# Local attention over windows of 64: q and k loaded as float32 by SyncE, transposed as float32 and cast when PSUM is emptied; 256 rows per transfer; manual program order

## The chip, the cores and the metric

One NeuronCore of a Trainium2 chip. The metric is device time in microseconds (us), the median of several executions; lower is better. One core runs alone. (Mean granted TensorE clock: the share of the full clock that the profile shows as granted.) The kernel before takes 966.62 us (966.24 to 967.0).

## The reference

```python
B, S, D, W = 4, 4096, 1536, 64            # q, k, v: float32, (B, S, D)
q_w, k_w, v_w = (x.reshape(B, S // W, W, D) for x in (q, k, v))
logits = einsum('bnwd,bnud->bnwu', q_w, k_w) * D ** -0.5
attn = softmax(logits)                    # over the last axis
out = einsum('bnwu,bnud->bnwd', attn, v_w).reshape(B, S, D)   # float32
```

The 16,384 rows are 128 blocks of 128 rows (two windows each). Whatever a kernel does, it must read 301.99 MB of q, k and v from HBM, the memory outside the core, and write 100.66 MB: 402.65 MB in all, 3.146 MB per block. SBUF and PSUM, below, are the core's own memories; in both kernels TensorE's results go to PSUM and are copied from there ("evicted") to SBUF.

## The kernel before

The parts that the change and the argument touch (pool lines shortened, cuts at "..."):

```python
inp = tile_pool(name="inp", bufs=3); outp = tile_pool(name="outp", bufs=6)
tp_ps = tile_pool(name="tp_ps", bufs=2, space=PSUM)
# lt_ps bufs=2, o_ps bufs=3, s_ps bufs=1

def load(blk):                       # 128 rows; float32 in HBM, float16 in SBUF: the transfer casts
    ...
    nc.gpsimd.dma_start(out=q16, in_=qb[blk].rearrange("p (c e) -> p c e", e=128))
    nc.gpsimd.dma_start(out=k16, in_=kb[blk].rearrange("p (c e) -> p c e", e=128))
    nc.gpsimd.dma_start(out=v16, in_=vb[blk])
    return q16, k16, v16
...
for blk in range(NBLK):
    ... load(blk) ...
    if len(pending_store) > 2:
        bs, ts = pending_store.pop(0)
        nc.gpsimd.dma_start(out=ob[bs], in_=ts)
    for g in range(3):               # 24 transposes: d onto the partitions
        tp = tp_ps.tile([128, 8, 128], FP16, tag="tp", name="tp")
        for i in range(8):
            ...
            nc.tensor.transpose(tp[:, i, :], src, ident)
        if g != 1:
            nc.vector.tensor_copy(out=xt[:, g * 8 : g * 8 + 8, :], in_=tp)
        else:
            nc.scalar.copy(out=xt[:, g * 8 : g * 8 + 8, :], in_=tp)
    # ... 12 score matmuls, exp on the two 64x64 diagonal tiles, row sums, reciprocal
    for j in range(D // 512):        # values, two 64-row matmuls side by side, then scaled into out_sb
        ...
```

All loads and stores (but the last three stores) go through one queue, GpSimd's. A scheduler orders the instructions.

The softmax here doesn't subtract the row's maximum and nothing guards it: scores larger than these inputs give would overflow.

Of the kernel before, what the change touches and what calls it, by code (L numbers as in the profile page):

```python
# [1 line left out]

# [4 lines left out]

FP16 = mybir.dt.float16
FP32 = mybir.dt.float32  # L10


@with_exitstack
def kernel(
    ctx: ExitStack,
    tc: tile.TileContext,
    q: bass.AP,
    k: bass.AP,
    v: bass.AP,
    out: bass.AP,  # L20
):
    nc = tc.nc

    B, S, D, W = q.shape[0], q.shape[1], q.shape[2], 64
    P = 128
    DC = D // 128
    NBLK = (B * S) // P
    scale = float(D) ** -0.5
    NPRE = 2

    qb = q.rearrange("b (n p) d -> (b n) p d", p=P)
    kb = k.rearrange("b (n p) d -> (b n) p d", p=P)
    vb = v.rearrange("b (n p) d -> (b n) p d", p=P)
    ob = out.rearrange("b (n p) d -> (b n) p d", p=P)

    consts = ctx.enter_context(tc.tile_pool(name="consts", bufs=1))
    inp = ctx.enter_context(tc.tile_pool(name="inp", bufs=3))
    xtp = ctx.enter_context(tc.tile_pool(name="xtp", bufs=2))
    etp = ctx.enter_context(tc.tile_pool(name="etp", bufs=2))
    outp = ctx.enter_context(tc.tile_pool(name="outp", bufs=6))  # L40
    rsp = ctx.enter_context(tc.tile_pool(name="rsp", bufs=2))

    tp_ps = ctx.enter_context(tc.tile_pool(name="tp_ps", bufs=2, space=bass.MemoryType.PSUM))
    lt_ps = ctx.enter_context(tc.tile_pool(name="lt_ps", bufs=2, space=bass.MemoryType.PSUM))
    o_ps = ctx.enter_context(tc.tile_pool(name="o_ps", bufs=3, space=bass.MemoryType.PSUM))
    s_ps = ctx.enter_context(tc.tile_pool(name="s_ps", bufs=1, space=bass.MemoryType.PSUM))

    exp_f = mybir.ActivationFunctionType.Exp
    copy_f = mybir.ActivationFunctionType.Copy

    def load(blk):
        q16 = inp.tile([128, DC, 128], FP16, tag="q16", name="q16")
        k16 = inp.tile([128, DC, 128], FP16, tag="k16", name="k16")
        v16 = inp.tile([128, D], FP16, tag="v16", name="v16")
        nc.gpsimd.dma_start(out=q16, in_=qb[blk].rearrange("p (c e) -> p c e", e=128))  # L55
        nc.gpsimd.dma_start(out=k16, in_=kb[blk].rearrange("p (c e) -> p c e", e=128))  # L56
        nc.gpsimd.dma_start(out=v16, in_=vb[blk])  # L57
        return q16, k16, v16

    pre = [load(blk) for blk in range(NPRE)]  # L60
    pending_store = []

    ident = consts.tile([128, 128], FP16, name="ident")
    ones = consts.tile([128, 8], FP16, name="ones")
    zeros = consts.tile([128, 1], FP32, name="zeros")
    nc.vector.memset(ident, 0.0)
    nc.vector.memset(ones, 1.0)
    nc.vector.memset(zeros, 0.0)
    nc.gpsimd.affine_select(
        out=ident,  # L70
        in_=ident,
        compare_op=mybir.AluOpType.not_equal,
        fill=1.0,
        base=0,
        pattern=[[-1, 128]],
        channel_multiplier=1,
    )

    for blk in range(NBLK):
        if blk < NPRE:  # L80
            q16, k16, v16 = pre[blk]
        else:
            q16, k16, v16 = load(blk)
        if len(pending_store) > 2:
            bs, ts = pending_store.pop(0)
            nc.gpsimd.dma_start(out=ob[bs], in_=ts)  # L86

        xt = xtp.tile([128, 2 * DC, 128], FP16, tag="xt", name="xt")
        for g in range(3):
            tp = tp_ps.tile([128, 8, 128], FP16, tag="tp", name="tp")  # L90
            for i in range(8):
                j = g * 8 + i
                c = j // 2
                src = q16[:, c, :] if (j % 2 == 0) else k16[:, c, :]
                nc.tensor.transpose(tp[:, i, :], src, ident)  # L95
            if g != 1:
                nc.vector.tensor_copy(out=xt[:, g * 8 : g * 8 + 8, :], in_=tp)  # L97
            else:
                nc.scalar.copy(out=xt[:, g * 8 : g * 8 + 8, :], in_=tp)  # L99

        lt = lt_ps.tile([128, 512], FP32, tag="lt", name="lt")
        for c in range(DC):
            nc.tensor.matmul(  # L103
                lt[:, 0:128],
                lhsT=xt[:, 2 * c + 1, :],
                rhs=xt[:, 2 * c, :],
                start=(c == 0),
                stop=(c == DC - 1),
            )

        et = etp.tile([128, 128], FP16, tag="et", name="et")
        nc.scalar.activation(  # L112
            et[0:64, 0:64], lt[0:64, 0:64], exp_f, bias=zeros[0:64], scale=scale
        )
        nc.scalar.activation(
            et[64:128, 64:128], lt[64:128, 64:128], exp_f, bias=zeros[64:128], scale=scale
        )

        sp = s_ps.tile([128, 8], FP32, tag="sp", name="sp")
        nc.tensor.matmul(  # L120
            sp[0:64, 0:1], lhsT=et[0:64, 0:64], rhs=ones[0:64, 0:1],
            tile_position=(0, 0), start=True, stop=True,
        )
        nc.tensor.matmul(  # L124
            sp[64:128, 0:1], lhsT=et[64:128, 64:128], rhs=ones[64:128, 0:1],
            tile_position=(64, 64), start=True, stop=True,
        )
        rs = rsp.tile([128, 1], FP32, tag="rs", name="rs")
        nc.vector.reciprocal(out=rs, in_=sp[:, 0:1])  # L129

        out_sb = outp.tile([128, D], FP32, tag="out_sb", name="out_sb")
        for j in range(D // 512):
            o = o_ps.tile([128, 512], FP32, tag="o", name="o")
            sl = slice(512 * j, 512 * (j + 1))
            nc.tensor.matmul(  # L135
                o[0:64, :], lhsT=et[0:64, 0:64], rhs=v16[0:64, sl],
                tile_position=(0, 0), start=True, stop=True,
            )
            nc.tensor.matmul(  # L139
                o[64:128, :], lhsT=et[64:128, 64:128], rhs=v16[64:128, sl],  # L140
                tile_position=(64, 64), start=True, stop=True,
            )
            if j % 2 == 0:
                nc.scalar.activation(out_sb[:, sl], o, copy_f, bias=0.0, scale=rs)  # L144
            else:
                nc.vector.tensor_scalar_mul(out_sb[:, sl], o, scalar1=rs)  # L146

        pending_store.append((blk, out_sb))

    for bs, ts in pending_store:  # L150
        nc.sync.dma_start(out=ob[bs], in_=ts)


# [1 line left out]
_INS = ['q', 'k', 'v']  # L155
_OUTS = [((4, 4096, 1536), 'float32')]


# [23 lines left out]
```

## Time and profile before

| | before |
|---|---|
| time, median | 966.62 us |
| profiled span, mean granted TensorE clock | 964.4 us, 0.632 |
| HBM bytes | 402.65 MB, 417 GB/s over the span |
| HBM bytes in the steady part, 100 to 900 us | 423.6 GB/s |
| last load landed | 955.8 us |

The steady rate is worked out from the trace's records of DMA packets: those that ended between 100 and 900 us, each counted at the size that it has in HBM. A packet is here one row of 1,536 values, moved by one of the 16 DMA engines. A packet of a casting load appears in the records with its float16 size, 3,072 bytes, and is counted as the 6,144 bytes that it reads. The table of stretches agrees: 265 GB/s at the SBUF side, and of the program's bytes 402.65 MB cross HBM for 251.66 MB at that side, so 265 x 1.6 = 424.

The page of the kernel before, its span, two rows of slices (each digit is a fortieth of the span; PEclk is the granted TensorE clock in tenths, DMA the busy share of the 16 DMA engines), the HBM line and the chain of waits:

```profile
span 964.4 us, 14246 instructions
...
PEclk9776575756756666566575755766656556565655
DMA  9999999999999999999999999999999999999997
...
HBM read 301.99 MB, written 100.66 MB: 417 GB/s over the span
...
DMA 94%; issue 4%; PE 1%; POOL 0%; DVE 0%; ACT 0%; POOLq 0%; ACTq 0%; DVEq 0%
DMA k<-in_k_dram 92%; DMA q<-in_q_dram 1%; PE tp L95 1%; DVE xt L97 0%; POOL q L55 0%; PE o L135 0%; PE lt L103 0%; PE o L139 0%; POOLq L56 0%; POOL v L57 0%; DVE out_sb L146 0%; ACT out_sb L144 0%; ACT et L112 0%; ACTq L177 0%; PE sp L120 0%
```

The digits of 9 say that the DMA engines are busy throughout, and the chain, followed back from the last instruction, goes from one k load to the next: the kernel waits for its data and for hardly anything else.

Three groups of instructions of the same page (count, then busy us and mean ns, then idle time of the engine just before and what ended it):

```profile
L95 PE MATMUL tp<-ident,q 128*128 128x128 f16 x1536 | 341.1, 296 | 28.8 <-DMA q<-in_q_dram 12.1
...
L97 DVE COPY xt<-tp 128x1024 f16<-128x1024 f16 x256 | 177.0, 691 | 392.4 <-PE tp L95 392.2
...
L99 ACT COPY xt<-tp 128x1024 f16<-128x1024 f16 x128 | 129.5, 1012 | 287.2 <-PE tp L95 287.2
```

And the DMA issues of that page (count, KB each, median us from issue to landing). The sizes of loads are those at the SBUF side, float16:

```profile
out_dram<-out_sb POOLq DMA_DIRECT2D x125, 768.0 KB, 14.2
q<-in_q_dram POOLq DMA_DIRECT2D x128, 384.0 KB, 14.3
k<-in_k_dram POOLq DMA_DIRECT2D x128, 384.0 KB, 14.3
v<-in_v_dram POOLq DMA_DIRECT2D x128, 384.0 KB, 14.3
```

Every kind of transfer takes the same 14.2 to 14.3 us; all stand in one queue in program order.

The timeline of the kernel before at 13.4 us, with the TensorE clock at full speed (start in us, then duration):

```profile
13.36 0.22 PE L95 MATMUL tp<-ident,q 128*128 128x128 f16 x1
...
13.42 0.22 PE L95 MATMUL tp<-ident,k 128*128 128x128 f16 x1
...
13.48 0.22 PE L95 MATMUL tp<-ident,q 128*128 128x128 f16 x1
```

Start to start, float16 transposes are 0.053 to 0.06 us apart. At the low clock (0.5 of the full one in the records, and granted for 74% of the span) the same timeline shows 0.107.

### The profile page before, as it was taken

To read this page: it belongs to the slowest core of one execution; us is meant where nothing else is said; L and a number is where in the kernel's file an instruction comes from. 1 tells how busy PE (TensorE), PEld (TensorE's weight loads), DVE (VectorE), ACT (ScalarE), POOL (GpSimd) and SP (SyncE) were. 2 spreads that over 40 slices of the span, in tenths; PEclk is the share of its full clock that TensorE was granted. 3 is DMA by queue.
4 is the path that set the end of the run, shared out by engine and by line. 5 is a ranking of instruction groups with operands and counts; after the bars stand their busy time and mean duration, and the time that the engine had idled before them with its cause. 6 is when DMAs were issued, how large, how long until landed. Compare 5 with 4: busy or idle time off the path is not lost.

```text
span 964.4 us, 14246 instructions
## 1 busy us (share of the span) xinstructions
PE 731.4 (76%) x5632; PEld 510.0 (53%) x5632; DVE 294.6 (31%) x515; ACT 378.1 (39%) x641; POOL 271.1 (28%) x514
## 2 busy tenths in 40 slices
PE   5667778787687877877878777777787777878775
PEld 3445555555455555555555555544555555555553
DVE  2323332333333333323233333323332323323332
ACT  3434343433333443434343433344343333344333
POOL 4222222222222222222222322322222222222220
PEclk9776575756756666566575755766656556565655
DMA  9999999999999999999999999999999999999997
GB/s 182 253 270 269 261 261 268 270 262 261 266 270 264 261 266 268 266 262 265 266 267 262 266 264 267 264 266 264 265 267 266 264 264 267 266 264 263 267 268 224
DMA packets 73795, 252.60 MB, mean 262 GB/s; under 512 B 8192, under 2 KB 8192, under 8 KB 73728
## 3 DMA queue, kind: packets, MB, share of 16 engines
q0 software_dynamic: 73296, 249.33, 104.6%
q1 hardware_dynamic: 432, 2.36, 0.6%
q8 instruction: 44, 0.72, 0.3%
q14 instruction: 23, 0.19, 0.0%
HBM read 301.99 MB, written 100.66 MB: 417 GB/s over the span
## 4 chain that ended last, share of the span: by engine, by line
DMA 94%; issue 4%; PE 1%; POOL 0%; DVE 0%; ACT 0%; POOLq 0%; ACTq 0%; DVEq 0%
DMA k<-in_k_dram 92%; DMA q<-in_q_dram 1%; PE tp L95 1%; DVE xt L97 0%; POOL q L55 0%; PE o L135 0%; PE lt L103 0%; PE o L139 0%; POOLq L56 0%; POOL v L57 0%; DVE out_sb L146 0%; ACT out_sb L144 0%; ACT et L112 0%; ACTq L177 0%; PE sp L120 0%
## 5 line engine op out<-in xcount | busy, mean ns | idle before, releaser
L95 PE MATMUL tp<-ident,k 128*128 128x128 f16 x1536 | 327.7, 305 | 139.6 <-DMA k<-in_k_dram 139.6
L95 PE MATMUL tp<-ident,q 128*128 128x128 f16 x1536 | 341.1, 296 | 28.8 <-DMA q<-in_q_dram 12.1
L95 PEld LDWEIGHTS <-k 128*128 128x128 f16 x1536 | 205.9, 139 | 205.3 <-DMA k<-in_k_dram 167.9
L97 DVE COPY xt<-tp 128x1024 f16<-128x1024 f16 x256 | 177.0, 691 | 392.4 <-PE tp L95 392.2
L95 PEld LDWEIGHTS <-q 128*128 128x128 f16 x1536 | 199.8, 137 | 89.8 <-DMA q<-in_q_dram 50.9
L99 ACT COPY xt<-tp 128x1024 f16<-128x1024 f16 x128 | 129.5, 1012 | 287.2 <-PE tp L95 287.2
L144 ACT ACTIVATE out_sb<-o,rs 128x512 f32<-128x512 f32 x256 | 168.6, 685 | 98.7 <-PE o L139 95.1
L103 PE MATMUL lt<-xt 128*128 128x128 f16 x1536 | 192.9, 295 | 3.0 <-DVE xt L97 1.8
L103 PEld LDWEIGHTS <-xt 128*128 128x128 f16 x1536 | 150.6, 136 | 27.4 <-DVE xt L97 26.5
L135 PE MATMUL o<-v,et 64*64 64x512 f16 x384 | 150.6, 502 | 0.0
L139 PE MATMUL o<-v,et 64*64 64x512 f16 x384 | 144.6, 498 | 0.0
L57 POOL DMA_DIRECT2D v<-in_v_dram x128 | 67.9, 530 | 178.1 <-DMA v<-in_v_dram 135.0
L86 POOL DMA_DIRECT2D out_dram<-out_sb x125 | 67.2, 537 | 173.5 <-DMA out_dram<-out_sb 134.0
L112 ACT ACTIVATE et<-lt,zeros 64x64 f16<-64x64 f32 x128 | 39.6, 309 | 192.4 <-PE lt L103 192.4
L56 POOL DMA_DIRECT2D k<-in_k_dram x128 | 67.9, 530 | 162.6 <-DMA k<-in_k_dram 162.6
L55 POOL DMA_DIRECT2D q<-in_q_dram x128 | 68.0, 531 | 156.2 <-PE o L139 124.0
L146 DVE TENSOR_SCALAR out_sb<-o,rs 128x512 f32<-128x512 f32 x128 | 96.0, 750 | 46.6 <-PE o L139 45.1
L129 DVE RECIPROCAL rs<-sp 128x1 f32<-128x1 f32 x128 | 21.5, 168 | 225.5 <-PE sp L124 221.0
L120 PE MATMUL sp<-ones,et 64*64 64x1 f16 x128 | 25.3, 198 | 56.5 <-ACT et L112 56.5
L120 PEld LDWEIGHTS <-et 64*64 64x64 f16 x128 | 14.4, 113 | 86.7 <-ACT et L112 86.2
L139 PEld LDWEIGHTS <-et 64*64 64x64 f16 x384 | 39.4, 132 | 16.8 <-issue 9.8
L135 PEld LDWEIGHTS <-et 64*64 64x64 f16 x384 | 43.5, 126 | 0.4
(12 smaller groups left out, 81.5 us busy)
## 6 DMA issues: line engine op xcount, KB each, us to landing
out_dram<-out_sb POOLq DMA_DIRECT2D x125, 768.0 KB, 14.2
q<-in_q_dram POOLq DMA_DIRECT2D x128, 384.0 KB, 14.3
k<-in_k_dram POOLq DMA_DIRECT2D x128, 384.0 KB, 14.3
v<-in_v_dram POOLq DMA_DIRECT2D x128, 384.0 KB, 14.3
out_dram<-out_sb SPq DMA_DIRECT2D x3, 768.0 KB, 7.8
```

The source lines that it names most:

```text
L55: nc.gpsimd.dma_start(out=q16, in_=qb[blk].rearrange("p (c e) -> p c e", e=128))
L56: nc.gpsimd.dma_start(out=k16, in_=kb[blk].rearrange("p (c e) -> p c e", e=128))
L57: nc.gpsimd.dma_start(out=v16, in_=vb[blk])
L86: nc.gpsimd.dma_start(out=ob[bs], in_=ts)
L95: nc.tensor.transpose(tp[:, i, :], src, ident)
L97: nc.vector.tensor_copy(out=xt[:, g * 8 : g * 8 + 8, :], in_=tp)
L99: nc.scalar.copy(out=xt[:, g * 8 : g * 8 + 8, :], in_=tp)
L103: nc.tensor.matmul(lt[:, 0:128], lhsT=xt[:, 2 * c + 1, :], rhs=xt[:, 2 * c, :], start=(c == 0), stop=(c == DC - 1),)
L135: nc.tensor.matmul(o[0:64, :], lhsT=et[0:64, 0:64], rhs=v16[0:64, sl], tile_position=(0, 0), start=True, stop=True,)
L139: nc.tensor.matmul(o[64:128, :], lhsT=et[64:128, 64:128], rhs=v16[64:128, sl], tile_position=(64, 64), start=True, stop=True,)
L144: nc.scalar.activation(out_sb[:, sl], o, copy_f, bias=0.0, scale=rs)
L146: nc.vector.tensor_scalar_mul(out_sb[:, sl], o, scalar1=rs)
```

## The change

The intent: take the cast out of DMA and q and k off GpSimd's software queue, make transfers twice as large, and lay down the order by hand, with the values of one block after the scores of the next. Its core (cut at "..."):

```diff
+BODY_G, BODY_R = 2, 1        # groups of 128 rows per transfer, rows per partition
+PREFETCH = 3
-    inp = ctx.enter_context(tc.tile_pool(name="inp", bufs=3))
-    outp = ctx.enter_context(tc.tile_pool(name="outp", bufs=6))
+    inp = ctx.enter_context(tc.tile_pool(name="inp", bufs=PREFETCH + 1))
+    outp = ctx.enter_context(tc.tile_pool(name="outp", bufs=3))
...
-        nc.gpsimd.dma_start(out=q16, in_=qb[blk].rearrange("p (c e) -> p c e", e=128))
-        nc.gpsimd.dma_start(out=k16, in_=kb[blk].rearrange("p (c e) -> p c e", e=128))
-        nc.gpsimd.dma_start(out=v16, in_=vb[blk])
+    ctx.enter_context(tc.manual_schedule())
+    def load(u):
+        for name, src in (("q", qf), ("k", kf), ("v", vf)):
+            dt = FP16 if name == "v" else FP32
+            t = inp.tile([P, LR, D], dt, tag=name + "in", name=name + "in")
+            ...
+            eng = nc.gpsimd if name == "v" else nc.sync
+            eng.dma_start(out=dst, in_=dram(src, u))
...
-    ident = consts.tile([128, 128], FP16, name="ident")
+    ident = consts.tile([P, P], FP32, name="ident")
...
-            tp = tp_ps.tile([128, 8, 128], FP16, tag="tp", name="tp")
+        per = 4 // (2 * R)
+        for c0 in range(0, DC, per):
+            tp = tp_ps.tile([P, per, 2, R, P], FP32, tag="tp", name="tp")
+            ...                                  # 4 transposes, float32
+            if flip[0] % 2 == 0:
+                nc.vector.tensor_copy(out=dst, in_=tp)      # casts to float16
+            else:
+                nc.scalar.copy(out=dst, in_=tp)
...
+    def store(i):
+        ...
+        nc.gpsimd.dma_start(out=dram(of, u), in_=src)
+    for i, u in enumerate(units):               # 63 units of 256 rows, then 2 of 128
+        if i + PREFETCH < N:
+            load(units[i + PREFETCH])
+        for g in range(u.G):
+            et = finish_scores(scores(u, g))
+            if prev is not None:
+                pi, pg, pet = prev
+                values(units[pi], pg, pet, False)
+                if pg == units[pi].G - 1:
+                    store(pi)
+            prev = (i, g, et)
```

The value matmuls also become one of full height (the softmax tile has zeros off its diagonal) instead of a pair of half height.

## The prediction

> **What bounds the kernel now.** DMA. The chain of waits gives 94% of the 964.4 us span to DMA, nearly all k loads; the slices show the 16 DMA engines 90% busy or more in all but the last. The program moves 402.65 MB (301.99 read, 100.66 written): 417 GB/s over the span. In the steady part the chain advances 14.83 us per two blocks of 128 rows (6.29 MB): 424 GB/s, 7.42 us per block. 64 x 14.83 = 949 us are that stream; some 15 us are start, end and a few hiccups of 0.7 us. The Trainium skill, "DMA: Bandwidth & Descriptors", Bandwidth, has 425 GB/s for the largest measured load and a ceiling of 435.2; the trace is at the first. 402.65 MB at 435.2 GB/s would be 925 us.
>
> **What the change leaves.** The same 402.65 MB cross HBM. The float16 cast only halved what arrived in SBUF (the page's 252.6 MB); that should rise to about 353 MB. The 424 GB/s counts the wide side of each transfer, so I take that side as the limit: giving up the halving costs nothing. Transfers are twice as large and fewer. GpSimd's DMA instructions (509, 0.53 us each, never the limit) fall to about 130. Gain: 0 to 1%.
>
> **What it adds.**
> - TensorE: 24 float32 transposes per block for 24 float16 ones. The timeline shows the latter 0.107 us apart at the low clock, 0.053 at the full one; mean granted clock 0.63. The Trainium skill, "TensorE: Matmul & The Clock Gate", Terms, calls transpose mode 4x faster for FP32, so I assume one pass; its Weight-path section denies float32 the fast weight load, so I allow up to twice the float16 spacing. Estimate per block at the low clock: transposes 2.6 (as now) to 5.1 us, 12 score matmuls 1.3, three full-height value matmuls 1.3, one wait for the last eviction 0.7: 5.9 to 8.5 us; at the full clock 3.5 to 4.8. The limit is 7.42. If TensorE becomes dense its clock should rise, so this stays hidden.
> - Evictions: six 128x512 float32 per block instead of three 128x1024 float16. From the groups, VectorE takes 0.75 us and ScalarE 0.685 us for a 128x512 float32 read of PSUM. VectorE goes from 2.3 to about 3.2 us per block, ScalarE from 2.95 to 4.0. Both below 7.42.
> - Values run one block behind scores, so TensorE no longer waits for exp (56 us idle now, not critical).
>
> **On the critical path:** almost nothing; these changes lie under the DMA stream. Start and end may give 0 to 5 us (the last block stores in thirds).
>
> **Predicted time: 957 us, range 940 to 1010.** Faster by over 2%: 0.13. Within 2%: 0.65. Slower by over 2%: 0.22.
>
> **What would show it.** The chain over 85% DMA, on qin or kin; DMA digits of 9; HBM 417 to 425 GB/s; SBUF-side traffic near 353 MB; float32 transposes spaced 0.053 to 0.21 us; VectorE and ScalarE busy about 400 and 520 us; TensorE waiting for loads in each unit.
>
> **What would make it wrong.** (1) A float32 transpose costs four float16 ones (over 0.2 us at the full clock): TensorE needs over 8 us per block, 1050 us or more, the chain transposes and evictions. (2) The clock stays low although TensorE is dense, and weight loads don't overlap: near 1090 us. (3) SyncE's uncast stream runs below 424 GB/s, or the doubled SBUF writes contend: 970 to 1000 us, DMA still leading. (4) The cast was what held DMA below 435 GB/s: 935 to 945 us.

## More of the kernel before

The end of the kernel before, from the table of stretches (span of the stretch; then for PE, PEld, DVE, ACT and POOL busy us and count; then granted clock, DMA share, GB/s):

```profile
950.00:955.00 5.00, 2.60 (x20) 1.46 (x17) 1.02 (x2) 1.37 (x2) 0.00 (x0) 0.50 0.83 255
955.00:960.00 5.00, 3.66 (x32) 2.36 (x29) 2.03 (x4) 2.62 (x5) 0.00 (x0) 0.82 0.30 121
960.00:965.00 5.00, 0.00 (x0) 0.00 (x0) 0.00 (x0) 0.27 (x1) 0.00 (x0) 0.53 0.39 157
```

## The result, and the profile after

The changed kernel takes 977.62 us (977.24 to 978.0) against 966.62. The ratio is 1.0113 (95% interval 1.0093 to 1.0132): 1.1% slower. Ratios here are the mean time of one kernel's runs over that of the kernel before's runs of the same rounds, so not quite the ratio of the medians that are quoted.

| | before | after |
|---|---|---|
| time, median | 966.62 us | 977.62 us |
| profiled span, mean granted clock | 964.4 us, 0.632 | 976.2 us, 0.907 |
| steady HBM rate, 100 to 900 us | 423.6 GB/s | 420.4 GB/s |
| all bytes at that rate | 952.9 us | 960.0 us |
| the rest: DMA not at that rate at start and end | 11.5 us | 16.2 us |

The last two rows divide the span. "All bytes" are all packets of the records (403.6 MB, instructions included), divided by the steady rate; the rest is the span less that. So 7.1 us of the 11.8 us came from the rate and 4.7 us from the ends.

The page after: span, slices, the two DMA queues that matter (packets, MB at the SBUF side, share of 16 engines), the HBM line and the chain:

```profile
span 976.2 us, 13049 instructions
...
PEclk9989899987988899889989989898998998898999
DMA  9999999999999999999999999999999999999995
...
q1 hardware_dynamic: 35280, 202.12, 50.9%
q0 software_dynamic: 34704, 150.22, 50.5%
...
HBM read 301.99 MB, written 100.66 MB: 412 GB/s over the span
...
ACT 0%; ACTq 0%
```

DMA is still at 9 in all slices but the last, and at 412 GB/s instead of 417. The bytes are now in two queues of nearly equal share. The chain says nothing this time: followed back from the last instruction it breaks off at once (its rows are all 0%), so what bounds the kernel has to be read from the slices and from waits. The granted clock rose to about 0.9. Runs 2 and 1 below differ in the float32 form alone and have 0.805 and 0.908, so part of the rise comes with the longer float32 transposes; the rest came with the order and the larger units (run 8, run 2 with 128 rows, has 0.664).

The groups that answer to those of before:

```profile
L142 PE MATMUL tp<-ident,kin 128*128 128x128 f32 x1536 | 431.6, 306 | 158.4 <-DMA kin<-in_k_dram 158.4
L142 PE MATMUL tp<-ident,qin 128*128 128x128 f32 x1536 | 430.6, 304 | 8.6 <-DMA qin<-in_q_dram 8.0
L147 DVE CAST xt<-tp 128x512 f16<-128x512 f32 x384 | 265.4, 691 | 435.6 <-PE tp L142 435.6
L149 ACT CAST xt<-tp 128x512 f16<-128x512 f32 x384 | 224.8, 585 | 446.7 <-PE tp L142 446.7
```

TensorE waits 158.4 us for k loads, its longest wait. Evictions are six per block instead of three, 691 and 585 ns each. VectorE is busy 381 us and ScalarE 460, far below the span.

The DMA issues:

```profile
qin<-in_q_dram SPq DMA_DIRECT2D x63, 1536.0 KB, 41.6
kin<-in_k_dram SPq DMA_DIRECT2D x63, 1536.0 KB, 47.7
out_dram<-out_sb POOLq DMA_DIRECT2D x63, 1536.0 KB, 20.4
vin<-in_v_dram POOLq DMA_DIRECT2D x63, 768.0 KB, 14.4
```

Now a store lands 20.4 us after its issue and a k load takes 47.7.

The timeline at the full clock and, second, at the low one:

```profile
501.11 0.27 PE L142 MATMUL tp<-ident,kin 128*128 128x128 f32 x1
...
501.22 0.27 PE L142 MATMUL tp<-ident,qin 128*128 128x128 f32 x1
...
501.33 0.27 PE L142 MATMUL tp<-ident,kin 128*128 128x128 f32 x1
```

```profile
509.60 0.42 PE L142 MATMUL tp<-ident,kin 128*128 128x128 f32 x1
...
509.81 0.42 PE L142 MATMUL tp<-ident,qin 128*128 128x128 f32 x1
```

Float32 transposes are 0.11 us apart at the full clock and 0.21 at the low one, twice the float16 spacing.

The end of the changed kernel:

```profile
950.00:955.00 5.00, 4.18 (x37) 3.06 (x33) 2.96 (x5) 3.12 (x7) 0.72 (x1) 1.00 0.70 290
955.00:960.00 5.00, 4.22 (x37) 3.16 (x38) 2.28 (x5) 3.35 (x7) 0.00 (x0) 1.00 0.52 211
960.00:965.00 5.00, 4.00 (x35) 2.71 (x33) 2.95 (x5) 3.14 (x7) 0.72 (x1) 1.00 0.00 0
965.00:970.00 5.00, 3.60 (x24) 1.75 (x24) 2.36 (x5) 3.63 (x8) 0.48 (x1) 1.00 0.77 315
970.00:977.00 7.00, 0.00 (x0) 0.00 (x0) 0.08 (x1) 0.38 (x1) 0.08 (x1) 0.70 0.58 225
```

From 960 to 965 us no byte moves while TensorE, VectorE and ScalarE work: the loads are done, the earlier stores are done, and the last blocks still have to be computed. The last k load landed at 954.8 us, that of the last 256-row unit at 943.6.

### The profile page after: what moved, and what is told of

Same layout as the page of the kernel before. It is cut to its first block, busy times and chain, and to the rows that moved or that the text cites. A ratio compares the mean times of both kernels' runs of the same rounds, so it can differ in the third digit from the quotient of the medians.

```text
span 976.2 us, 13049 instructions
## 1 busy us (share of the span) xinstructions
PE 690.7 (71%) x5120; PEld 505.1 (52%) x5120; DVE 381.3 (39%) x645; ACT 459.8 (47%) x897; POOL 92.7 (9%) x134
## 5 line engine op out<-in xcount | busy, mean ns | idle before, releaser
L142 PE MATMUL tp<-ident,kin 128*128 128x128 f32 x1536 | 431.6, 306 | 158.4 <-DMA kin<-in_k_dram 158.4
L142 PE MATMUL tp<-ident,qin 128*128 128x128 f32 x1536 | 430.6, 304 | 8.6 <-DMA qin<-in_q_dram 8.0
L147 DVE CAST xt<-tp 128x512 f16<-128x512 f32 x384 | 265.4, 691 | 435.6 <-PE tp L142 435.6
L149 ACT CAST xt<-tp 128x512 f16<-128x512 f32 x384 | 224.8, 585 | 446.7 <-PE tp L142 446.7
L142 PEld LDWEIGHTS tp<-ident,kin 128*128 128x128 f32 x1536 | 244.7, 159 | 184.9 <-DMA kin<-in_k_dram 180.0
L128 PE MATMUL lt<-xt 128*128 128x128 f16 x1536 | 234.3, 238 | 111.3 <-DVE xt L147 80.1
L142 PEld LDWEIGHTS tp<-ident,qin 128*128 128x128 f32 x1536 | 243.9, 159 | 23.9 <-issue 8.0
L86 POOL DMA_DIRECT2D vin<-in_v_dram x65 | 46.2, 711 | 806.3 <-PE o L200 793.2
L200 PE MATMUL o<-vin,et 128*128 128x512 f16 x384 | 103.5, 377 | 0.5 <-ACT out_sb L206 0.5
L194 DVE RECIPROCAL rs<-sp 128x1 f32<-128x1 f32 x128 | 21.5, 168 | 118.9 <-PE sp L189 118.9
L200 PEld LDWEIGHTS <-et 128*128 128x128 f16 x384 | 28.1, 96 | 15.9 <-issue 0.6
L189 PEld LDWEIGHTS <-et 128*128 128x128 f16 x128 | 12.5, 98 | 0.6 <-ACT et L179 0.6
## 6 DMA issues: line engine op xcount, KB each, us to landing
qin<-in_q_dram SPq DMA_DIRECT2D x63, 1536.0 KB, 41.6
kin<-in_k_dram SPq DMA_DIRECT2D x63, 1536.0 KB, 47.7
out_dram<-out_sb POOLq DMA_DIRECT2D x63, 1536.0 KB, 20.4
```

The source lines that it names most:

```text
L86: eng.dma_start(out=dst, in_=dram(src, u))
L128: nc.tensor.matmul(lv[:, r, :, :], lhsT=xt[:, c, 1, r, :], rhs=xt[:, c, 0, :R, :], start=(c == 0), stop=(c == DC - 1),)
L142: nc.tensor.transpose(tp[:, c - c0, x, r, :], src[:, g * R + r, c * P : (c + 1) * P], ident)
L147: nc.vector.tensor_copy(out=dst, in_=tp)
L149: nc.scalar.copy(out=dst, in_=tp)
L189: nc.tensor.matmul(sp[:, t, 0:1], lhsT=et[:, r, t, :], rhs=ones[:, 0:1], start=(r == 0), stop=(r == R - 1),)
```

## The experiments

Two losses had to be explained: 3.2 GB/s of the steady rate, and 4.7 us at the ends. Theories of the rate: P, an uncast packet is slower than a cast one; Q (later H), SyncE's hardware queue is slower; M, two queues taking turns cost it; C, only v's cast packets lose something when they take turns with another queue's. Theories of the ends: T, coarse units and slow blocks; B, the backlog that two queues leave. In the tables, "ends" is the span less all bytes at the run's steady rate, as above. The record of expectations speaks of a "tail", which is last load landed to the end of the span. Rate and ends come from one profiled execution of each kernel; kernels that differ only in PSUM buffers, depth or a GpSimd copy agree within 0.1 GB/s (the changed kernel, runs 12 and 14: 420.3 to 420.4; runs 1 and 13: 424.6 and 424.7).

Sixteen kernels ran, all correct, each timed in three rounds beside the kernel before. They ran on four chips, on which the kernel before took 966.4 to 966.7 us.

### 1. One queue: q and k float32, issued by GpSimd

```diff
-            eng = nc.gpsimd if name == "v" else nc.sync
+            eng = nc.gpsimd
```

> The changed kernel with one thing altered: q and k, still float32, are issued by GpSimd like v and the stores; nothing is left to SyncE but the last stores. The changed kernel's steady stream (100 to 900 us) carries 420 GB/s of HBM bytes, the kernel before 424. Theory P (an uncast 6 KB packet is itself a little slower than a cast one, whoever issues it): the rate stays at 420 to 421 and the time at 975 to 980 us. Rival Q (SyncE's hardware queue, or two queues taking turns, costs the rate): the rate returns to 423 to 424 and the time falls to 968 to 972. Neither expects the tail (last load landed to the end, 21 us) to change by more than 2 us.

962.10 us against 966.38, ratio 0.9954 (0.9939 to 0.9969); rate 424.6 GB/s, ends 9.3 us. One line undoes both losses: 15.5 us less than the changed kernel's median, and faster than the kernel before. The float32 loads and transposes stayed. P falls, as far as q and k go: uncast they run at 424.6. Q seemed right. That the ends shrank too, no theory had expected.

### 2. Float16 again, in the changed kernel's order

```diff
-            dt = FP16 if name == "v" else FP32
+            dt = FP16
-            eng = nc.gpsimd if name == "v" else nc.sync
+            eng = nc.gpsimd
-    ident = consts.tile([P, P], FP32, name="ident")
+    ident = consts.tile([P, P], FP16, name="ident")
-        per = 4 // (2 * R)
-            tp = tp_ps.tile([P, per, 2, R, P], FP32, tag="tp", name="tp")
+        per = 8 // (2 * R)
+            tp = tp_ps.tile([P, per, 2, R, P], FP16, tag="tp", name="tp")
```

> The changed kernel's program order, 256-row transfers and buffers, but q and k cast to float16 by GpSimd's queue again, float16 transposes, eight to a PSUM bank, three evictions per block. Theory P and rival Q both expect the steady rate back at 423 to 424 GB/s. Theory T (the longer tail comes of 256-row units and of a TensorE that needs 5.7 us per block, because six evictions per block pass through two PSUM banks): blocks at the end take under 5 us, the tail falls from 21 to 17 or 18 us, the time to 964 to 968 us. If the order itself, not the data type, made the tail, it stays 21 us and the time is 969 to 972.

958.80 us, ratio 0.9919 (0.9904 to 0.9934); rate 425.4, ends 8.5 us. Faster than expected. Beside run 1 it shows what the float32 form by itself costs in one queue: 0.8 GB/s and 0.8 us at the ends, 3.3 us of time. And it shows that the order and the large transfers are a gain, which the split of the queues hid.

### 3. The kernel before with the data type and queue alone changed

```diff
-        q16 = inp.tile([128, DC, 128], FP16, tag="q16", name="q16")     # k16 likewise
-        nc.gpsimd.dma_start(out=q16, ...)
+        q16 = inp.tile([128, DC, 128], FP32, tag="q16", name="q16")
+        nc.sync.dma_start(out=q16, ...)
-        for g in range(3):                # 8 transposes into float16
+        for g in range(6):                # 4 transposes into float32
```

> The kernel before with only the data type and queue changed: q and k float32 by SyncE, 128 rows per transfer, float32 transposes, six evictions per block; scheduler, buffers and order as before. Theories P and Q expect the steady rate of the changed kernel, 420 to 421 GB/s, so 7 us more than before. Theory T expects a tail of 11 to 14 us, not 21. Together 972 to 977 us. If the data type did everything, 976 to 980 with a tail near 20.

975.25 us, ratio 1.0095 (1.0079 to 1.0111); rate 419.8, ends 12.4 us. As expected: the loss of rate belongs to data type and queue, whatever the order, and most of the longer ends does not.

### 4. The changed kernel with 128 rows per transfer

```diff
-BODY_G, BODY_R = 2, 1
-PREFETCH = 3
+BODY_G, BODY_R = 1, 1
+PREFETCH = 6
```

(and six output buffers)

> The changed kernel with 128 rows per transfer instead of 256 and twice as many units ahead (six), so the same bytes in flight. Theory T expects the last load to be followed by two blocks of work at most: tail 13 to 16 us instead of 21, time 969 to 973 us, steady rate unchanged at 420 to 421 GB/s. If large transfers helped the rate, it falls below 420 and the time stays at 975 to 980.

976.79 us, ratio 1.0104 (1.0088 to 1.0121); rate 420.1, ends 14.8 us. A miss. The tail did shorten, from 21.5 to 16.6 us (958.9 to 975.5), but the last load landed 4 us later. T falls as the main cause: smaller units alone don't repair the ends.

### 5. Stores on SyncE's queue, behind the loads

```diff
-        nc.gpsimd.dma_start(out=dram(of, u), in_=src)
+        nc.sync.dma_start(out=dram(of, u), in_=src)
```

> The changed kernel with the body's stores moved from GpSimd's queue to SyncE's, behind the q and k loads: SyncE's hardware queue now carries 75% of the HBM bytes instead of 50%, GpSimd's only v. The first four runs settled that the rate hangs on the queue: 424.6 GB/s with none of the body on the hardware queue, 420.4 with half. Theory H (the hardware queue is the slower one by itself): a line through those two points gives 418.3 GB/s at 75%. Theory M (two queues taking turns on the same engines cost it): the smaller share is now 25%, so about half of the loss, 422 to 423. Theory B (the tail is a matter of backlog: with stores behind the loads in one queue, loads land early and stores are left to fill the end) expects last load to end as in the run with one queue, and idle DMA at the ends down from about 16 us to 9 or 10. So H: 970 to 973 us; M: 962 to 966.

972.53 us, ratio 1.0061 (1.0044 to 1.0077); rate 420.2, ends 10.3 us. H fails (it said 418.3) and so does M (422 to 423): three quarters on the hardware queue are no worse than half. B holds: the rate did not move and the ends lost 5.9 us. The DMA issues and the end of this run:

```profile
qin<-in_q_dram SPq DMA_DIRECT2D x63, 1536.0 KB, 33.2
kin<-in_k_dram SPq DMA_DIRECT2D x63, 1536.0 KB, 33.1
out_dram<-out_sb SPq DMA_DIRECT2D x63, 1536.0 KB, 33.0
vin<-in_v_dram POOLq DMA_DIRECT2D x63, 768.0 KB, 12.5
```

```profile
950.00:955.00 5.00, 4.20 (x37) 3.14 (x38) 2.27 (x4) 3.37 (x7) 0.00 (x0) 1.00 0.82 342
955.00:960.00 5.00, 4.00 (x35) 2.71 (x34) 2.96 (x5) 3.12 (x7) 0.00 (x0) 1.00 0.48 196
960.00:965.00 5.00, 3.63 (x24) 1.78 (x24) 2.33 (x5) 3.62 (x8) 0.00 (x0) 1.00 0.64 261
965.00:970.00 5.00, 0.00 (x0) 0.00 (x0) 0.10 (x1) 0.40 (x1) 0.00 (x0) 0.84 0.81 315
```

Stores now land after 33.0 us instead of 20.4, loads after 33.1 to 33.2 instead of 41.6 and 47.7. The k load of the last 256-row unit lands at 935.2 us instead of 943.6. So stores are left over for the time in which the last blocks are computed, and the stretch without a byte is gone.

### 6. Only k on SyncE's queue

```diff
-            eng = nc.gpsimd if name == "v" else nc.sync
+            eng = nc.sync if name == "k" else nc.gpsimd
```

> The changed kernel with q moved to GpSimd's queue, so that SyncE's hardware queue carries k alone, 25% of the HBM bytes. Theories H and M both expect 422 to 423 GB/s here; it tests that the loss is graded at all. If any use of the second queue costs the whole loss, 420. Time 965 to 972 us.

967.61 us, ratio 1.0013 (0.9998 to 1.0028); rate 422.8, ends 11.5 us. The loss is graded, as both theories said.

### 7. Everything on SyncE's queue

v is loaded as float32 too and cast by GpSimd in SBUF; depth of two units so that it fits.

```diff
-PREFETCH = 3
+PREFETCH = 2
-            dt = FP16 if name == "v" else FP32
-            eng = nc.gpsimd if name == "v" else nc.sync
+            dt = FP32
+            eng = nc.sync                    # and the stores
+        nc.gpsimd.tensor_copy(out=u.v16[:, :n, :], in_=u.v[:, :n, :])     # once per unit
```

> Everything on SyncE's hardware queue: v is loaded as float32 too and cast to float16 by GpSimd in SBUF, stores are issued by SyncE, two units ahead instead of three so that it fits SBUF. One queue, no cast in DMA, same HBM bytes. Theory H: the line gives 416 GB/s at 100%, so about 970 us of stream, 978 to 982 in all. Theory M: one queue alone does not alternate, 424 GB/s or more, 958 to 964 us. In the packet lengths, 47% of the hardware queue's 6 KB packets took 247 ns in the changed kernel and the rest 234; H expects most to take 247 here, M nearly all 234.

971.23 us, ratio 1.0050 (1.0035 to 1.0065); rate 420.3, ends 8.9 us. H (416) and M (424) both miss, and so do both forecasts of the packet lengths: 46% of the 6 KB packets took 234 ns, hardly any took 247 (0.1%), and 53% took 235 to 246. B holds again: one queue, short ends.

### 8. Run 2 with 128 rows per transfer

```diff
-BODY_G, BODY_R = 2, 1
-PREFETCH = 3
+BODY_G, BODY_R = 1, 1
+PREFETCH = 6
```

> The fastest run so far (float16 cast by GpSimd in the changed kernel's order, 958.8 us, rate 425.4) with 128 rows per transfer and six units ahead. Its idle DMA at start and end was about 8.5 us; smaller units may take 1 to 3 us of that: 956 to 958 us, rate 425. If 256-row transfers are what raised the rate from 423.6 to 425.4, the rate falls to 423.6 to 424 and the time is 959 to 962.

964.82 us, ratio 0.9983 (0.9968 to 0.9998); rate 423.7, ends 10.4 us. The second alternative held for the rate, though the time came out above it. In one queue, 256-row transfers are worth 1.7 GB/s; 423.7 is the rate of the kernel before, which also has 128 rows.

### 9 and 10. No cast in DMA at all: one queue, and two

Run 9 is run 7 with all loads and stores on GpSimd's queue; run 10 is run 7 with q and k on SyncE's and v and the stores on GpSimd's, the changed kernel's split.

```diff
-            eng = nc.sync                    # run 7
+            eng = nc.gpsimd                                         # run 9, stores too
+            eng = nc.gpsimd if name == "v" else nc.sync             # run 10, stores nc.gpsimd
```

> The run with everything on SyncE's queue (971.2 us, 420.3 GB/s, nothing cast in DMA), with the one difference that loads and stores are issued by GpSimd instead. So far both theories missed: the rate is 424.6, 422.8, 420.4, 420.2, 420.3 GB/s for 0, 25, 50, 75, 100% of the bytes on the hardware queue, which falls no further past one half. Combined theory HM: the hardware queue by itself costs about 1% and taking turns adds up to 0.5% more. It expects 424 to 425 GB/s here, 959 to 963 us. If instead the missing cast or the depth of two units made the 420.3, the rate stays at 420 to 421 and the time near 970.

> The same program with q and k on SyncE's queue and v and the stores on GpSimd's: the changed kernel's split of half and half, but nothing is cast in DMA (GpSimd casts v in SBUF, as in the run before). In the changed kernel about as many 6 KB packets of the hardware queue (12,800 of 27,400 in the steady part) took 247 ns as there were cast packets of v (13,600); with one queue only the first of each run of packets behind a cast one does. If the extra loss of taking turns comes of alternating with cast packets (theory C), it is gone here: 422 to 423 GB/s, and few packets of 247 ns. If any alternation costs it (theory M), 420.0 to 420.5 GB/s and the long packets remain. Theory B expects the idle DMA at the ends as in the changed kernel, 14 to 16 us: 968 to 971 us (C) or 973 to 977 us (M).

Run 9: 972.25 us, ratio 1.0059 (1.0044 to 1.0074); rate 420.4, ends 10.4 us. Run 10: 974.97 us, ratio 1.0085 (1.0070 to 1.0100); rate 421.2, ends 15.3 us. Run 9 ends H and its blend HM: with everything on GpSimd's queue and nothing cast, the rate is that of everything on SyncE's. Run 10 ends M: without casts, two queues are no slower than one. C's direction is right (the packets of about 247 ns are gone from their place) but its number, 422 to 423, was not. B holds: the split makes long ends again.

### 11. Towards the fastest: two neighbouring rows per partition

Run 2 with packets of 12 KB in HBM, at the cost of twice the score and value matmuls.

```diff
-BODY_G, BODY_R = 2, 1
+BODY_G, BODY_R = 1, 2
```

> An attempt to beat both kernels, from the fastest run so far (float16 cast by GpSimd, 256-row transfers, 958.8 us): two neighbouring rows per partition, so that every packet reads or writes 12 KB of HBM instead of 6, at the cost of twice the score and value matmuls. A 6 KB packet takes 234 ns[...]: if the rest is a fixed cost per packet, the rate rises to 428 to 430 GB/s and the time falls to 948 to 953 us; if it scales with bytes, rate 425 to 426 and 957 to 961 us.

953.02 us, ratio 0.9860 (0.9845 to 0.9875); rate 428.7, ends 10.5 us. "The rest" in the expectation is what a packet takes beyond moving its bytes; a figure for that had no source in this case and is cut. The first alternative held, with the time at its edge. A 12 KB store packet takes 460 ns, less than two of 234, so a part of a packet's time does not grow with its bytes. It is the fastest kernel and beats both.

### 12. Three PSUM buffers for transposes, two for outputs

```diff
-    tp_ps = ... bufs=2        o_ps = ... bufs=3
+    tp_ps = ... bufs=3        o_ps = ... bufs=2
```

> The changed kernel with three PSUM banks for transposes and two for the outputs (before: two and three). Theory B says that in the changed kernel the last four blocks, each 5.7 us of TensorE and evictions, lie bare after the k load of the last 256-row unit; a shorter block shortens the end in proportion. With a third bank, a block should take 4.8 to 5.3 us, so 2 to 4 us less: 973.5 to 975.5 us, steady rate unchanged at 420.4. If the end is set by DMA, no change: 977 to 978.

978.96 us, ratio 1.0127 (1.0110 to 1.0144); rate 420.4, ends 17.2 us. A miss of the means: from the k load of the last 256-row unit to the last transpose, four blocks, it took 25.0 us (941.6 to 966.6) instead of 22.6, so the blocks got longer, not shorter, with two output buffers. The time did follow them, but as a test of B it is weak.

### 13 and 14. Controls: v cast by the transfer, with the depth and the GpSimd copy of runs 7, 9 and 10

```diff
-PREFETCH = 3
+PREFETCH = 2
+        nc.gpsimd.tensor_copy(out=u.v16[:, :n, :], in_=u.v[:, :n, :])     # v is float16 already
```

applied to run 1 (13) and to the changed kernel (14).

> Control, one queue with cast: q, k (float32), v (cast to float16 by the transfer) and stores all on GpSimd's queue, with the depth of two units and a GpSimd copy of v in SBUF that the three uncast runs had. Theory C: steady rate 424 to 425 GB/s as in the run without these two additions, against 420.4 with v uncast; 961 to 965 us. If depth or the GpSimd copy made the 420.4, it is 420 to 421 here as well; 970 to 973 us.

> Control, two queues with cast: the changed kernel with the same depth of two and the same GpSimd copy. Theory C: 420 to 420.6 GB/s and again some 12,000 to 13,000 packets of the hardware queue at 247 ns in the steady part; 975 to 980 us. If the additions matter, the rate leaves 420.4 by more than 0.8.

Run 13: 961.11 us, ratio 0.9945 (0.9930 to 0.9960); rate 424.7, ends 9.1 us. Run 14: 976.01 us, ratio 1.0100 (1.0085 to 1.0116); rate 420.3, ends 15.0 us. Both as C expected: depth and copy are not the cause. With 9 and 10 they make a table of two by two under equal conditions (steady GB/s of HBM bytes; q and k always float32):

| | v uncast | v cast by its transfer |
|---|---|---|
| one queue (runs 9, 13) | 420.4 | 424.7 |
| two queues, q and k on SyncE's (runs 10, 14) | 421.2 | 420.3 |

The stretch from 100 to 900 us of these four runs, 9, 13, 10 and 14 in this order. The last number is GB/s at the SBUF side, to be multiplied by 402.65 / 352.3 = 1.143 where v is cast:

```profile
100.00:900.00 800.00, 577.82 (x4253) 423.19 (x4253) 316.56 (x531) 380.66 (x743) 298.75 (x266) 0.90 1.02 420
...
100.00:900.00 800.00, 580.17 (x4306) 425.60 (x4304) 320.18 (x537) 384.85 (x752) 300.77 (x270) 0.90 1.03 372
...
100.00:900.00 800.00, 579.37 (x4255) 425.35 (x4256) 316.56 (x531) 380.69 (x743) 222.26 (x159) 0.89 1.02 421
...
100.00:900.00 800.00, 577.46 (x4249) 424.57 (x4249) 316.98 (x532) 381.02 (x744) 222.29 (x160) 0.89 1.03 368
```

Casting v is worth 1% in one queue and nothing in two. The queue split costs 1% if v is cast and nothing if it isn't.

The packet records show where. Of the packets of 6,144 bytes that started between 100 and 900 us, most take 234 ns; some of those near a cast packet take 247:

| run | share of bytes on SyncE's queue | cast packets | 6 KB packets of 244 to 259 ns | rate |
|---|---|---|---|---|
| 1 | 0 | 13,853 | 1,031 | 424.6 |
| 6 | 25% | 13,731 | 6,071 | 422.8 |
| the changed kernel | 50% | 13,651 | 12,818 | 420.4 |
| 5 | 75% | 13,563 | 12,824 | 420.2 |

In one queue the v packets of an engine come in runs of 16, and there is about one long packet per run (13,853 / 16 = 866). In the changed kernel and run 5 nearly every v packet has a long neighbour, and all the long ones but seven are SyncE's (in run 6, 5,236 of the 6,071). 11,787 more packets of 13 ns more on 16 engines are 9.6 us in 800; the rate of the changed kernel against run 1 costs 8.0 us in 800.

The records don't name the engine, but they let it be followed: nearly every packet starts 3 or 4 ns before another one ends, or 15 to 19 ns where that one is a cast packet, so ends can be paired with starts. Paired so in the changed kernel, 12,693 of SyncE's long packets follow a cast packet on their engine, and the engine starts its next packet 243.5 ns after a long one, 230.6 after one of 234 ns and 228.2 after a cast one. So the 13 ns are time of the engine, not an overlap of the records.

The uncast runs lose about as much in another way. In run 9, 53% of the packets take 235 to 246 ns, and the mean from start to start is 232.9 ns; in run 1, 6% of the 6 KB packets do, and the means are 231.1 ns after a 6 KB packet and 229.6 after a cast one. In run 10, 41% do. That the changed kernel and run 9 both have 420.4 GB/s is thus two different losses of one size.

### 15. The changed kernel with 12 KB packets

```diff
-BODY_G, BODY_R = 2, 1
+BODY_G, BODY_R = 1, 2
```

> The changed kernel, queues and float32 loads as they are, with two neighbouring rows per partition, so 12 KB packets. That gave the one-queue float16 form 425.4 to 428.9 GB/s. If the cost of alternating is one fixed time per cast packet (13 ns), it halves with the number of packets: rate 424.5 to 426, and with the float32 evictions as before the ends stay bare: 966 to 970 us. If it grows with the packet, 423 to 424 and 969 to 973 us.

959.67 us, ratio 0.9929 (0.9915 to 0.9944); rate 427.0, ends 12.9 us. Better than either alternative. The long packets are still there, 473 ns against 460: again 13 ns, for packets of twice the size, and half as many of them (6,082 of SyncE's 13,874). So the 13 ns are half the share of a packet's time.

### 16. Run 11 with six output buffers

```diff
-    outp = ctx.enter_context(tc.tile_pool(name="outp", bufs=3))
+    outp = ctx.enter_context(tc.tile_pool(name="outp", bufs=6))
```

> The fastest run so far (953.0 us) with six output buffers instead of three: near its end ScalarE and VectorE wait for output buffers whose stores lie behind the last loads in the queue (waits of 0.9 to 2.3 us on stores), while the DMA share falls to 0.69 and 0.42. With six they don't wait, and the last stores are issued 3 to 5 us earlier: 949 to 951 us, steady rate unchanged at 428.9.

953.66 us, ratio 0.9866 (0.9849 to 0.9882); rate 428.8, ends 11.0 us. A miss: the last stores were issued 4 us earlier and landed at 950.0 instead of 950.8 us, and the span stayed at 952. The waits for output buffers near the end cost nothing.

## Why the prediction was wrong

The prediction of the time, 957 us, was wrong in its direction: the kernel became 1.1% slower. Its range, 940 to 1010, holds 977.62, and "within 2%" was given 0.65; but the range was wide enough for a gain and a loss alike, and the step below that gave its sign failed, so that much was luck.

1. **"What bounds the kernel now. DMA."** Right, before and after: digits of 9 in both, and TensorE waits for kin 158 us after.
2. **TensorE stays hidden.** Right. The float32 transposes are 0.11 us apart at the full clock and 0.21 at the low one, the upper end of the spacing allowed, and the clock rose from 0.632 to 0.907. VectorE and ScalarE were predicted at about 400 and 520 us and are at 381 and 460. Run 1 keeps all of this on-chip work and is faster than the kernel before.
3. **"I take that side as the limit: giving up the halving costs nothing. ... Gain: 0 to 1%."** This is the step that failed. The bytes were counted right (353 MB at the SBUF side, 402.65 at HBM) and 420.4 GB/s came of them, not 424 or more. The wide side alone does not set the rate: the same HBM bytes in one queue run at 425.4 GB/s with all loads cast (run 2), 424.6 with v alone cast (run 1) and 420.4 with none (run 9). Giving up the cast of q and k costs 0.2%; what costs 1% is that the split takes from the one cast that is left, v's, what it gives, as runs 9, 10, 13 and 14 show: behind nearly every cast packet SyncE's next one takes 13 ns longer. The prediction had not asked what the second queue does; it was counted only as fewer instructions for GpSimd. Its own point (3) of what could go wrong, "SyncE's uncast stream runs below 424 GB/s, or the doubled SBUF writes contend: 970 to 1000 us, DMA still leading", named the outcome, but neither of its two causes is the one found: SyncE's queue is no slower than GpSimd's for the same uncast bytes (420.3 and 420.4), and run 1, with the same doubled SBUF writes for q and k, runs at 424.6.
4. **"Start and end may give 0 to 5 us."** This failed too: they cost 4.7 us. The Trainium skill, "DMA: Bandwidth & Descriptors", Queues, rings and completion order, says that each DMA engine goes round between the queue rows it has work for, packet by packet. The trace agrees: with ends paired with starts as above, about 25,500 of GpSimd's 27,200 data packets in the steady part of the changed kernel are followed on their engine by one of SyncE's, and 640 by another of GpSimd's. (That SyncE's queue had 210.3 of the 420.4 GB/s and GpSimd's 209.2 says nothing of it: the program puts half of its bytes on each.) So stores, which in one queue stand behind the loads, take their half of the engines as soon as they are issued. In the steady part the place of the stores is neutral (420.2 in run 5, 420.4 here). At the end it is not: the stores are already done, the loads come late, and the last blocks are computed with nothing left to move. The ends were 14.8 to 17.2 us with q and k on one queue and the stores on the other, with 256 rows or 128, v cast or not (the changed kernel, runs 4, 10, 12, 14); 8.5 to 10.4 us for 6 KB packets with one queue, or with the stores behind the loads (runs 1, 2, 5, 7, 8, 9, 13). The pattern is not the whole of it: the kernel before, one queue in its own order, has 11.5, run 3, the split in that order, 12.4, and run 6, with k alone split off, 11.5. Run 5 is the direct test: one changed line, same rate, 5.9 us less.
5. **Larger transfers.** They are worth something in one queue: 425.4 against 423.7 GB/s (runs 2 and 8). In the split kernel they are worth almost nothing: 420.4 against 420.1 (the changed kernel and run 4).

Open: why a 6 KB packet takes 13 ns longer behind a cast packet, and why, when v is not cast, half of the packets take a few ns longer. The uncast runs write more at the SBUF side (402 MB against 353), which may be the reason of the second, but no run tests it. That the packets follow cast ones on the same engine, and the engines' turns, are inferred by pairing times, not read from a record. The split of the ends by cause rests on run 5 and on the pattern, not on a count of bytes left over.

## What to carry to other kernels

In a kernel bound by DMA, a second queue need not be free even when it issues less and moves the same bytes. Here it cost 1% of the rate beside a queue that cast (and none where nothing was cast), and it changed which transfers stand behind which, which cost about 5 us at the end. In this kernel one queue for loads and stores avoided both; putting the stores behind the loads gave back the end alone. Look at the last 20 us of the table of stretches for a stretch without bytes. When the rate itself is the limit, try longer packets: two neighbouring rows per partition gave 428.7 GB/s instead of 425.4 and made the fastest kernel, 953 us.

## What the Trainium skill lacked or had wrong

- "DMA: Bandwidth & Descriptors", Rules for kernel authors, says of spreading DMAs over SP, ACT and GpSimd for bandwidth that it "Doesn't help" and only saves issue time. Here it can also cost: 424.6 to 420.4 GB/s when q and k moved to SyncE's queue beside a casting queue, and 5.9 us at the end that came back when the stores joined the loads.
- The same page says which queue may cast, not what a cast does to the rate. In one queue, with equal HBM bytes: 425.4 GB/s with all loads cast, 424.6 with v alone, 420.4 with none.
- The same page's Bandwidth section, under "Why small descriptors are slow (HBM only)", gives a fixed overhead of about 3 cycles per packet, with an example of 256 bytes, and compares no packets of several KB. Here packets of 12 KB still gained on 6 KB at the same transfer size: 428.7 against 425.4 GB/s in one queue, 427.0 against 420.4 in two.
- "TensorE: Matmul & The Clock Gate", Terms, has transpose mode "4× faster for FP32" without a time. Here float32 transposes of 128x128 are 0.11 us apart at the full clock, twice the float16 spacing of 0.053 to 0.06.
- The same page, Part 4, says that the full clock doesn't engage for transpose mode. Here transposes did run at the full clock, float32 ones 0.11 us apart, in a kernel in which 24 of the 40 matmuls of a block are transposes and the mean granted clock was 0.907. Whether transposes alone would raise the clock, no run shows.
